# Selection of a gathered tile's experts, moved from the end of the routing into the sweep

## The chip, the cores and the metric

The kernel runs on one core of one Trainium2 chip. The metric is the device time of one execution in microseconds, the median of several runs. TensorE (PE), VectorE (DVE), ScalarE (ACT), GpSimd (POOL) and SyncE (SP) each work through their own instructions in order and wait for one another by semaphores. Weights and tables lie in HBM and come in by DMA, mostly issued on SP's queue; POOL issues the indirect ones.

## The reference, cut to what matters

Two layers, each with four token mixers and then the PEER retrieval, on 256 latent and 256 context tokens of width 1024. PEER is the part that the change touches. Each of 8 heads scores two lists of 128 keys, takes the 16 best of each, forms the 256 sums, takes the 16 best of these and so names 16 of 16384 experts:

```python
def peer(x, wq, keys, u_tab, v_tab):
    t, d = x.shape
    q = (x @ wq).astype(f32).reshape(t, PEER_HEADS, 2, PEER_DK // 2)
    s = jnp.einsum('thpd,hpnd->thpn', q, keys.astype(f32))
    sv, si = lax.top_k(s, PEER_TOPK)
    cand = (sv[:, :, 0, :, None] + sv[:, :, 1, None, :]).reshape(t, PEER_HEADS, PEER_TOPK * PEER_TOPK)
    cidx = (si[:, :, 0, :, None] * PEER_NKEYS + si[:, :, 1, None, :]).reshape(t, PEER_HEADS, PEER_TOPK * PEER_TOPK)
    best, pos = lax.top_k(cand, PEER_TOPK)
    eidx = jnp.take_along_axis(cidx, pos, axis=-1)
    g = jax.nn.softmax(best, axis=-1)
    ...
        act = jax.nn.gelu(jnp.einsum('tkd,td->tk', u_tab[ec].astype(f32), xc.astype(f32)), approximate=False)
        return jnp.einsum('tk,tkd->td', gc * act, v_tab[ec].astype(f32))
```

## The kernel before, in words

Layer 0 has four tiles of 128 tokens. Three of them (384 tokens) go through a dense **sweep** over all 128 blocks of 128 experts: for block j, `u_mm` (L1262) multiplies the tokens with U's block j (24 matmuls, tile names `wh`, `wl`, outputs `po`) and applies Gelu (L1278) into a tile `ga`; `gate` multiplies `ga` by the routing weights G and splits it into `Wh` and `Wl`; `split_v` splits V's block, loaded as `vr`, into `vh` and `vl`; `v_mm` adds the block's 18 products into `mm` and `at` (L1698). Every fp32 operand is a sum of a high part, copied by ACT, and a low part, subtracted by DVE, both in `halves` (L1246); `Wh`, `vh`, `wh` are ACT's, `Wl`, `vl`, `wl` DVE's (L1247, L1248). `wl` and `wh` have 3 buffers each, `vr` has 2, `vh` and `vl` 3, `Wh` and `Wl` 4.

The fourth tile, tile 0, goes through a **gather** (L1311): 128 indirect DMAs from POOL (L1321) fetch one row of U for each of its tokens, by the indices `gix`, into three buffers `grow`, DVE takes the dot product of each row with its token (L1328), and after a Gelu 128 rows of V are gathered and summed (L1330, L1332). The generator `gather` yields after each row. In the sweep, loop j calls it a fixed number of times behind `late`, the DVE split of block j+1's V, so that the rows stand in DVE's queue between the splits.

Ahead of both lies the **routing** (L1599): queries, the lists of the 16 best (`top16`), then per tile `select` and `scatter`. `select(i)` (L1434) yields six times: `lst` (ACT, L1439), the candidates' sums `cand` (DVE, L1442), the best 16 of each head `best` and `pos` (four yields), positions into `ab2`, an Exp on ACT (L1473), then `match` against the numbers `iotar`, twice (L1478 to L1483), and for tile 0 the indices `gix` and weights `gw` (L1493 to L1495). `scatter` makes one-hot operands (`ohA`, `ohB`, `ohC`) and PE builds the weights G block by block (L1560); ACT evacuates them to `gblk` and SP stores them to `gd` (L1564), from where the sweep loads them as `G` (L1664). While the routing runs, U steps of the sweep are worked ahead (`early`, a filler).

Routing of layer 0 ends with the scatter of the last dense tile and, in the kernel before, with tile 0's select:

```python
                fill.add(early(ne))
                if NG:
                    yield from select(0)
```

The tile pool `tk` (L1363) closes with the routing and its memory goes to the sweep's tiles; the pool `sel` stays open in layer 0. What order the instructions take on each engine is decided by a scheduler from the program's order, the buffers and its own estimates; the program's order with `issue_after` is the hand that sets it here. Layer 1 has no gathered tile.

Of the kernel before, what the change touches and what calls it, by code (L numbers as in the profile page):

```python
# [10 lines left out]
F16 = mybir.dt.float16  # L11
# [8 lines left out]
P = 128  # L20
# [253 lines left out]
def body(ctx, tc, I, out, dbg=None):  # L274
# [311 lines left out]
    for l in range(DEPTH):  # L586
# [641 lines left out]
        NG = 0 if last else 1  # L1228
# [66 lines left out]
        def early(upto):  # L1295
            while nu[0] < upto:
                u_next()
                yield
# [58 lines left out]
        gath = gather() if NG else iter(())  # L1357

        g_first = (acc if NG else up.tile([P, NB * 64], F32, name="gfirst"))[:, :NB * 64].rearrange("p (b j t) -> p b j t", j=2, t=32)
        with ExitStack() as tx:  # L1360

            sel = (px if NG else tx).enter_context(tc.tile_pool(name=f"sel{l}", bufs=2))
            tk = tx.enter_context(tc.tile_pool(name=f"tk{l}", bufs=1))  # L1363
# [6 lines left out]
            gparts = gT.bitcast(F16).rearrange("p (t s) -> p t s", s=2)  # L1370
            iota4 = tk.tile([P, P, 4], F16, name="iota4")
            dve.tensor_copy(iota4, iota[:, :, None].to_broadcast([P, P, 4]))
            iotar = tk.tile([P, 16, 8], F16, name="iotar")
            dve.tensor_copy(iotar, iota[:, :16, None].to_broadcast([P, 16, 8]))
            KEYS = tk.tile([P, 1024], F32, name="keys")
            pool.dma_start(KEYS, I['keys'][l])
# [18 lines left out]
            def queries(h, a):  # L1395

                w = un.next('wq')
                ps = mm_tile()
                sl = slice(a - nt, a - nt + 256)
                for k in range(KD):  # L1400
                    o = k * 128
                    mm3(ps[:, :256], (w[0][:, o:o + 128], w[1][:, o:o + 128]), (nh[:, k, sl], nl[:, k, sl]), k == 0, k == KD - 1)
                act.activation(q_of(h, a), ps[:, :256], AF.Copy)
# [169 lines left out]
            def both(a, b, na):  # L1573

                live = True
                for _ in b:
                    for _ in range(na):
                        if live:
                            live = next(a, 0) is None
                    yield  # L1580
                for z, _ in enumerate(a):
                    if z % 3 == 2:
                        yield

            def chain(*gens):
                for g in gens:
                    yield from g

            def queries_of(a):
                for u in range(8):  # L1590
                    queries(u, a)
                    if u % 2:
                        yield
# [5 lines left out]
            def routing():  # L1599


                tiles = (0, 1) if last else (2, 3, 1)
                for u in range(0, 8, 2):
                    queries(u, 256)
                    queries(u + 1, 256)
                    if last and u == 6:
                        fill.add(early(own))
                    yield from lists(tiles[:1 if last else 2], (u, u + 1))
                if last:
                    per_step[0] = 2  # L1610
                    yield from select(0)

                    def rest():
                        yield from lists((1,), range(8))
                        fill.add(early(ne))
                        yield from select(1)
                else:
                    yield from both(queries_of(0), select(2), 1)

                    fill.add(early(own + 2048 // nd))  # L1620
                lo_eng[0] = dve
                for z in range(1, ND):
                    more = lists((tiles[z + 1],), range(8)) if z + 1 < ND else iter(())
                    yield from both(scatter(tiles[z - 1]), rest() if last else chain(select(tiles[z]), more), 3)
                per_step[0] = 1

                v0[:] = [up.tile([P, D], F32, name="grow", bufs=3) for _ in range(3)]
                sp.dma_start(v0[0], I['V'][l, 0])
                end = scatter(tiles[-1], True)
                others = lists((0,), range(8)) if NG else iter(())  # L1630
                for z, _ in enumerate(end):
                    next(others, 0)
                    if z == 8:
                        fill.add(early(ne - 2 if NG else ne))
                    yield
                fill.add(early(ne))
                if NG:
                    yield from select(0)

            for _ in routing():  # L1640
                for _ in range(per_step[0]):
                    fill.step()
            fill.flush()


        with ExitStack() as dx:
# [8 lines left out]
            def load_v(j):  # L1655
                if j < P:
                    vr[j] = dp.tile([P, D], F32, name="vr", bufs=2) if j else v0[0]
                    if j:
                        sp.dma_start(vr[j], I['V'][l, j])
# [73 lines left out]
            for j in range(P):  # L1733
                load_v(j + 2)
                load_g(j + 4)

                while nu[0] < min(P, j + own + (ne - own) * max(0, 64 - j) // 64) and free:
                    u_next()
                gate(j + 1)
                if j == 80:  # L1740
                    assert last or all(z < own for z, _ in gas.values())
                    if last:
                        htok = fin.tile([P, 2, D], F32, name="htok")
                        sp.dma_start(htok, h2.rearrange("q p d -> p q d"))
                    else:
                        sp.dma_start(hT, h2)
                        hT_back.append(j)
                late = split_v(j + 1)
                if j < P - TAIL:
                    for i in range(ND):  # L1750
                        v_mm((j,), i, range(2))
                if last and j >= 40 and j % 4 == 0:
                    next(mrows, 0)
                if last and j == 116:
                    table_for_rstd()
                if last and j == 100:

                    rws = fin.tile([P, 2, D], F32, name="rws")
                    grow = fin.tile([KD, P], F32, name="grow8")
                    ps = mm_tile()  # L1760
                    transpose(ps[:KD, :P], mod[:, 40:48, 1])
                    act.activation(grow, ps[:KD, :P], AF.Copy)
                    grow_d = dr.tile([KD, P], F32, name="grow_d")
                    pool.dma_start(grow_d, grow)
                    for q, x in enumerate((grow_d, I['FG'])):
                        pool.dma_start(rws[:, q], bass.AP(tensor=x.tensor, offset=x.offset, ap=[[0, P], [1, D]]))
                if NG and j < P - 1:

                    with tc.issue_after(late.ins):
                        for _ in range((2 if j > 1 else 0) + (j > 24 and j % 2)):  # L1770
                            if next(gath, 0) is not None:
                                break
                        else:
                            continue
                        for _ in range(2):
                            next(mrows, 0)
# [75 lines left out]
```

## Time and profile before

| | |
|---|---|
| median of 3 runs | 3031.93 us (3028.62 to 3033.39) |
| profiled execution: its time, its span | 3033.08 us, 3031.3 us |
| PE busy | 2933.1 us, 97% |
| DVE busy | 2269.7 us, 75% |
| ACT busy | 1478.8 us, 49% |
| POOL busy | 530.7 us, 18% |
| HBM traffic over the span | 228 GB/s |

Times in the profile are microseconds from the span's start. The scatter of the last tile ends near 836; the sweep's V part of layer 0 begins at 849.59 and goes on to 1815. The profile names an instruction by its line, its engine, its operation and its tiles; what stands in square brackets behind a row is the time that the engine was idle before it, and what ended that.

### The profile page before, as it was taken

How to read it: one execution, taken by the hardware profiler on the slowest of the kernel's cores; microseconds unless marked ns; L12 is line 12 of the kernel's file. 1: busy time of each engine (PE TensorE's matmuls, PEld its weight loads, DVE VectorE, ACT ScalarE, POOL GpSimd, SP SyncE). 2: the span in 40 equal slices, each digit the busy share in tenths (PEclk: the TensorE clock that was granted, in tenths of full speed). 3: DMA queues.
4: the chain of work that ended last, by engine and by line, in shares of the span. 5: the costliest groups of instructions: out<-in, count | busy, mean ns of one | idle time of the engine just before them, and what ended most of it. 6: DMA issues, size and time to landing. Idle time of an engine off the chain costs nothing.

```text
span 3031.3 us, 47486 instructions
## 1 busy us (share of the span) xinstructions
PE 2933.1 (97%) x17500; PEld 2590.3 (85%) x17500; DVE 2269.7 (75%) x4818; ACT 1478.8 (49%) x2603; POOL 530.7 (18%) x394
## 2 busy tenths in 40 slices
PE   8999999998999999999999998999899999999997
PEld 6877777898889999999999986789898988999985
DVE  5765988799878777777787687888699667555545
ACT  5444533559843333333333335465558654555543
POOL 1001100230034444444444102000150000000000
PEclk9999999999999999999999999999999999999999
DMA  7232578556689988988989754367546699766644
GB/s 274 73 104 81 182 232 269 185 189 222 240 297 346 317 314 304 323 321 307 326 305 319 263 187 147 90 194 221 191 147 215 209 305 308 220 209 209 214 141 146
DMA packets 271673, 693.42 MB, mean 229 GB/s; under 512 B 22440, under 2 KB 115120, under 8 KB 270928
## 3 DMA queue, kind: packets, MB, share of 16 engines
q1 hardware_dynamic: 228096, 534.85, 52.9%
q0 software_dynamic: 43344, 155.54, 14.9%
q8 instruction: 137, 2.24, 0.3%
q14 instruction: 96, 0.79, 0.1%
HBM read 630.53 MB, written 59.77 MB: 228 GB/s over the span
## 4 chain that ended last, share of the span: by engine, by line
PE 74%; DVE 13%; DMA 7%; ACT 3%; issue 3%; POOL 0%; SPq 0%; DVEq 0%; ACTq 0%; POOLq 0%
PE mm L1698 12%; PE at L1698 12%; PE po L405 9%; PE po L407 9%; PE po L406 8%; PE mm L405 5%; PE mm L407 5%; PE mm L406 5%; PE at L1560 3%; DMA wraw<-in_W_dram 2%; DMA vr<-in_V_dram 2%; DMA wraw<-in_U_dram 1%; PE at L401 1%; DVE wl L337 1%; DMA grow<-in_UR_dram,gix 1%
## 5 line engine op out<-in xcount | busy, mean ns | idle before, releaser
L405 PE MATMUL po<-nh,wh 128*128 128x384 f32 (+1 forms) x2048 | 637.8, 311 | 4.7 <-ACT wh L1247 2.2
L407 PE MATMUL po<-nh,wl 128*128 128x384 f32 (+1 forms) x2048 | 635.3, 310 | 3.3 <-DVE wl L1248 2.6
L1247 ACT ACTIVATE vh<-vr 128x1024 fp32r<-128x1024 f32 x254 | 269.8, 1062 | 369.2 <-DMA vr<-in_V_dram 339.9
L405 PEld LDWEIGHTS po<-nh,wh 128*128 128x128 f32 x2048 | 390.7, 191 | 14.1 <-ACT wh L1247 2.8
L407 PEld LDWEIGHTS po<-nh,wl 128*128 128x128 f32 x2048 | 390.2, 191 | 5.1 <-DVE wl L1248 3.5
L1248 DVE TENSOR_TENSOR vl<-vr,vh 128x1024 fp32r<-128x1024 f32 x254 | 310.5, 1222 | 110.8 <-ACT vh L1247 110.4
L1247 ACT ACTIVATE wh<-wraw 128x1024 fp32r<-128x1024 f32 x236 | 249.5, 1057 | 287.7 <-PE po L406 251.7
L1248 DVE TENSOR_TENSOR wl<-wraw,wh 128x1024 fp32r<-128x1024 f32 x221 | 269.6, 1222 | 115.0 <-ACT wh L1247 114.9
L405 PE MATMUL mm<-nh,wh 128*128 128x256 f32 (+1 forms) x1056 | 346.6, 330 | 8.0 <-ACT nh L502 3.9
L406 PE MATMUL po<-nl,wh 128*128 128x384 f32 x1024 | 343.7, 336 | 0.0
L407 PE MATMUL mm<-nh,wl 128*128 128x256 f32 (+1 forms) x1056 | 341.7, 325 | 0.8 <-POOL wl L337 0.4
L406 PE MATMUL mm<-nl,wh 128*128 128x256 f32 (+1 forms) x992 | 324.2, 328 | 1.4 <-DVE nl L429 1.2
L336 ACT ACTIVATE wh<-wraw 128x1024 fp32r<-128x1024 f32 x176 | 186.0, 1059 | 276.4 <-PE mm L406 89.8
L406 PE MATMUL po<-nh,wh 128*128 128x256 f32 x1024 | 290.9, 284 | 0.0
L1698 PE MATMUL mm<-vl,Wh 128*128 128x512 f32 x635 | 250.3, 394 | 6.3 <-DVE vl L1248 5.9
L1698 PE MATMUL mm<-vh,Wh 128*128 128x512 f32 x635 | 248.7, 392 | 1.4 <-ACT vh L1247 1.4
L1698 PE MATMUL at<-vh,Wl 128*128 128x512 f32 x635 | 248.5, 391 | 0.0
L1698 PE MATMUL at<-vh,Wh 128*128 128x512 f32 x635 | 248.2, 391 | 0.0
L1698 PE MATMUL mm<-vh,Wl 128*128 128x512 f32 x635 | 247.5, 390 | 0.0
L1698 PE MATMUL at<-vl,Wh 128*128 128x512 f32 x635 | 247.0, 389 | 0.0
L405 PEld LDWEIGHTS mm<-nh,wh 128*128 128x128 f32 x1056 | 203.2, 193 | 34.4 <-issue 5.9
L1332 DVE SCALAR_TENSOR_TENSOR gacc<-grow,gdot,gacc 128x1024 f32<-128x1024 f32 x127 | 162.9, 1283 | 92.5 <-DMA grow<-in_V_dram,gix 91.1
(369 smaller groups left out, 6279.2 us busy)
## 6 DMA issues: line engine op xcount, KB each, us to landing
wraw<-in_U_dram SPq DMA_DIRECT2D x276, 512.0 KB, 4.6
vr<-in_V_dram SPq DMA_DIRECT2D x254, 512.0 KB, 4.6
wraw<-in_W_dram SPq DMA_DIRECT2D x214, 512.0 KB, 3.8
gd<-gblk SPq DMA_DIRECT2D x80, 512.0 KB, 4.3
G<-gd SPq DMA_DIRECT2D x32, 768.0 KB, 7.9
G<-gd SPq DMA_DIRECT2D x32, 512.0 KB, 5.6
grow<-in_W_dram SPq DMA_DIRECT2D x24, 512.0 KB, 4.5
ulo<-wl SPq DMA_DIRECT2D x20, 512.0 KB, 3.6
```

Of the source, the lines that this page charges most:

```text
L336: act.activation(h, r, AF.Copy)
L337: (pool if order[m][1] == 'wq' or order[m][:2] == (1, 'na') and order[m][2] < 2 or order[m][0] == 0 and order[m][1] in ('gate', 'hyn') and ...
L401: pe.transpose(o, i, ident)
L405: pe.matmul(ps, w[0], x[0], start=first, stop=False)
L406: pe.matmul(ps, w[0], x[1], start=False, stop=False)
L407: pe.matmul(ps, w[1], x[0], start=False, stop=last)
L1247: act.activation(h, r, AF.Copy)
L1248: return eng.tensor_tensor(lo, r, h.bitcast(F32), op=ALU.subtract)
L1332: dve.scalar_tensor_tensor(acc, g, dot[:, e:e + 1], acc, op0=ALU.mult, op1=ALU.add)
L1560: pe.matmul(ps4[:, :, z], A[:, :, z], C[:, z, :, h], start=h == 1, stop=h == 0)
L1698: pe.matmul(accs[i][h], w[a][:, i * 128:(i + 1) * 128], v[b][:, h * 512:(h + 1) * 512], start=j == 0 and a + b == 0, stop=j == P - 1 and a ...
```

## The change

It moves tile 0's select out of the routing generator and puts it in front of the gather, as its first steps. The loop of the sweep, which calls the gather twice per block (three times for every other block from 25 on), did so from j = 2; now it does from j = 0, so that select's six yields fall to j = 0 to 2 and the gather begins at j = 3. `iotar`, which select reads, moves from the pool `tk` to `sel`.

```diff
@@ -1370,7 +1370,7 @@
-            iotar = tk.tile([P, 16, 8], F16, name="iotar")
+            iotar = sel.tile([P, 16, 8], F16, name="iotar", bufs=1)
@@ -1634,13 +1634,14 @@
                 fill.add(early(ne))
-                if NG:
-                    yield from select(0)
 
             for _ in routing():
                 for _ in range(per_step[0]):
                     fill.step()
             fill.flush()
+            if NG:
+
+                gath = chain(select(0), gath)
@@ -1767,7 +1768,7 @@
                     with tc.issue_after(late.ins):
-                        for _ in range((2 if j > 1 else 0) + (j > 24 and j % 2)):
+                        for _ in range(2 + (j > 24 and j % 2)):
                             if next(gath, 0) is not None:
```

How this moves instructions is seen at three places (from line 1645 on, lines of the changed kernel are one higher). The first is DVE at the start of the last dense tile's scatter. Before:

```order
L1442 TENSOR_TENSOR cand<-sv 128x8x16
L1383 MAX best<-cand 128x8 x2
L1384 MAX_INDEX pos<-best,cand 128x8
L1385 MATCH_REPLACE rep<-best,cand 128x60
L1384 MAX_INDEX pos<-best,cand 128x8
L1386 MAX best<-rep 128x8
L1383 MAX best<-cand 128x8
L1387 MAX_INDEX pos<-best,rep 128x8
L1384 MAX_INDEX pos<-best,cand 128x8
L1385 MATCH_REPLACE rep<-best,cand 128x60
L1522 TENSOR_TENSOR ohA<-iota_5725,iT 128x1024
L1514 TENSOR_SCALAR gT<-at 128x128
```

Now, at the same place:

```order
L1385 MATCH_REPLACE rep<-sv,mm 128x128
L1386 MAX sv<-rep 128x8
L1387 MAX_INDEX si<-sv,rep 128x8
L1522 TENSOR_TENSOR ohA<-iota_5725,iT 128x1024
L1514 TENSOR_SCALAR gT<-at 128x128
```

The candidates and first best lists of tile 0 no longer stand between tile 0's lists (`sv`, `si`) and the scatter's one-hot operands.

The second place is ACT, where the scatter's last blocks give way to the sweep. Before:

```order
L1562 ACTIVATE gblk<-at 128x128x4 x6
L1439 ACTIVATE lst<-si 128x256
L1562 ACTIVATE gblk<-at 128x128x4 x2
L1256 ACTIVATE wh<-wraw 128x1024
L1566 ACTIVATE gacc<-gblk 128x64
L1278 ACTIVATE hT<-po_9154 128x384
L1247 ACTIVATE wh<-wraw 128x1024 x2
L1473 ACT_TABLE_LOAD
L1473 ACTIVATE best<-best 128x128
L1278 ACT_TABLE_LOAD
L1278 ACTIVATE hT<-po_9196 128x384
L1247 ACTIVATE wh<-wraw 128x1024
```

Now:

```order
L1562 ACTIVATE gblk<-at 128x128x4 x7
L1256 ACTIVATE wh<-wraw 128x1024
L1562 ACTIVATE gblk<-at 128x128x4
L1278 ACTIVATE hT<-po_9135 128x384
L1566 ACTIVATE gacc<-gblk 128x64
L1247 ACTIVATE wh<-wraw 128x1024
L1247 ACTIVATE Wh<-ga 128x384 x2
L1439 ACTIVATE lst<-si 128x256
L1247 ACTIVATE wh<-wraw 128x1024
```

`wh` stands one evacuation earlier, `lst` behind the first two `Wh`, and the Exp with its table loads has left this stretch for one further on.

The third place is DVE's queue from the indices `gix` to the first gathered rows (L1328). Before:

```order
L1493 SCALAR_TENSOR_TENSOR gix<-ij 128x128
L1494 SCALAR_TENSOR_TENSOR gix<-ij 128x128
L1248 TENSOR_TENSOR vl<-vr,vh 128x1024
L1687 TENSOR_TENSOR ga<-ga,G_9298 128x384 x2
L1248 TENSOR_TENSOR wl<-wraw,wh 128x1024
L1248 TENSOR_TENSOR Wl<-ga,Wh 128x384
L1248 TENSOR_TENSOR vl<-vr,vh 128x1024
L1248 TENSOR_TENSOR Wl<-ga,Wh 128x384
L1687 TENSOR_TENSOR ga<-ga,G_9309 128x384
L1248 TENSOR_TENSOR wl<-wraw,wh 128x1024
L1248 TENSOR_TENSOR vl<-vr,vh 128x1024
L1328 SCALAR_TENSOR_TENSOR grow,gdot<-grow,mtok 128x1024 x2
```

Now, from the first gathered rows on (the `vl` ahead of them is V7's, the two in the piece are V8's and V9's, the `wl` is U27's):

```order
L1248 TENSOR_TENSOR vl<-vr,vh 128x1024
L1688 TENSOR_TENSOR ga<-ga,G_9502 128x384
L1248 TENSOR_TENSOR wl<-wraw,wh 128x1024
L1328 SCALAR_TENSOR_TENSOR grow,gdot<-grow,mtok 128x1024 x3
L1248 TENSOR_TENSOR Wl<-ga,Wh 128x384
L1248 TENSOR_TENSOR vl<-vr,vh 128x1024
L1328 SCALAR_TENSOR_TENSOR grow,gdot<-grow,mtok 128x1024
L1688 TENSOR_TENSOR ga<-ga,G_9502 128x384
L1328 SCALAR_TENSOR_TENSOR grow,gdot<-grow,mtok 128x1024
L1248 TENSOR_TENSOR Wl<-ga,Wh 128x384
L1328 SCALAR_TENSOR_TENSOR grow,gdot<-grow,mtok 128x1024
L1248 TENSOR_TENSOR vl<-vr,vh 128x1024
```

The gather's rows start behind V7's split instead of V3's, and they come closer together: behind V9's split two more rows, U27's `wl`, three rows with a gate and a `Wl` between, V10's split, two rows, U28's `wl`, one row and V11's split follow. The order on PE, DVE, ACT and SP away from the end of the routing and the sweep's first dozen blocks, and POOL's altogether, is the same as before.

## Rows read from the trace of the kernel before

**Rows 1.** The page: busy time of each engine, with its share and count.

```profile
PE 2933.1 (97%) x17500; PEld 2590.3 (85%) x17500; DVE 2269.7 (75%) x4818; ACT 1478.8 (49%) x2603; POOL 530.7 (18%) x394
```

**Rows 2.** Windows: span, length, busy PE, PEld, DVE, ACT, POOL; clock, DMA share, GB/s.

```profile
836.00:850.00 14.00, 10.39 (x61) 9.78 (x60) 13.08 (x43) 10.15 (x16) 0.00 (x0) 1.00 0.70 262
850.00:854.00 4.00, 4.00 (x12) 3.11 (x11) 4.00 (x11) 1.85 (x2) 0.00 (x0) 0.57 0.98 310
854.00:870.00 16.00, 16.00 (x77) 13.81 (x77) 8.42 (x12) 7.39 (x10) 10.78 (x3) 1.00 0.98 331
870.00:880.00 10.00, 10.00 (x52) 9.01 (x51) 7.47 (x12) 0.72 (x2) 4.92 (x4) 1.00 0.64 215
...
960.00:1800.00 840.00, 840.00 (x4248) 763.70 (x4247) 644.49 (x816) 299.30 (x410) 306.50 (x228) 1.00 0.87 305
```

**Rows 3.** PE's timeline: start, duration, engine, line, operation, tiles, [idle before, its releaser].

```profile
797.06 1.06 PE L1560 MATMUL at<-ohC,ohA 128*128 128x128 f16 x8 [1.43 <-DVE ohC L1538]
...
838.50 0.44 PE L405 MATMUL po<-nh,wh 128*128 128x384 f32 x1 [1.45 <-ACT wh L1256]
838.78 0.34 PE L406 MATMUL po<-nl,wh 128*128 128x384 f32 x1
838.95 0.34 PE L407 MATMUL po<-nh,wl 128*128 128x384 f32 x1
...
849.59 0.50 PE L1698 MATMUL mm<-grow,Wh 128*128 128x512 f32 x1 [2.15 <-ACT Wh L1247]
...
850.39 0.51 PE L1698 MATMUL at<-grow,Wh 128*128 128x512 f32 x1
...
854.04 0.40 PE L1698 MATMUL mm<-grow,Wh 128*128 128x512 f32 x1
854.27 0.39 PE L1698 MATMUL at<-grow,Wh 128*128 128x512 f32 x1
...
906.60 0.50 PE L1698 MATMUL mm<-vl,Wh 128*128 128x512 f32 x1 [1.43 <-DVE vl L1248]
```

**Rows 4.** DVE's timeline, the selection of tile 0, first step to last.

```profile
790.78 0.27 DVE L1442 TENSOR_TENSOR cand<-sv 128x128 f32<-128x128 f32 x1
...
841.57 0.22 DVE L1456 TENSOR_SCALAR sl<-pos 128x128 uint32<-128x128 uint32 x1
...
847.77 1.22 DVE L1478 TENSOR_TENSOR match<-iotar,ab 128x2048 f16<-128x2048 f16 x1
...
854.11 0.28 DVE L1494 SCALAR_TENSOR_TENSOR gix<-ij 128x128 int32<-128x128 f32 x1
```

**Rows 5.** ACT's timeline, from the scatter's end to the first Wh.

```profile
835.65 0.64 ACT L1439 ACTIVATE lst<-si 128x256 f16<-128x256 uint32 x1
...
837.40 1.05 ACT L1256 ACTIVATE wh<-wraw 128x1024 fp32r<-128x1024 f32 x1
...
849.02 0.94 ACT L1247 ACTIVATE Wh<-ga 128x384 fp32r<-128x384 f32 x2 [1.08 <-DVE match L1478]
```

**Rows 6.** POOL's timeline: the first indirect DMA and one further on.

```profile
854.47 8.86 POOL L1321 DMA_INDIRECT grow<-in_UR_dram,gix  x1 [48.75 <-DVE gix L1494]
...
907.96 1.68 POOL L1321 DMA_INDIRECT grow<-in_UR_dram,gix  x1 [8.54 <-DVE grow L1328]
```

**Rows 7.** DVE's timeline: last split before the gather, rows 1, 4 and 10.

```profile
861.20 1.22 DVE L1248 TENSOR_TENSOR vl<-vr,vh 128x1024 fp32r<-128x1024 f32 x1
...
870.67 1.23 DVE L1328 SCALAR_TENSOR_TENSOR grow<-grow,mtok 128x1024 f32<-128x1024 f32 x1 [8.25 <-DMA grow<-in_UR_dram,gix]
...
877.74 1.22 DVE L1328 SCALAR_TENSOR_TENSOR grow<-grow,mtok 128x1024 f32<-128x1024 f32 x1 [1.71 <-DMA grow<-in_UR_dram,gix]
...
895.77 1.22 DVE L1328 SCALAR_TENSOR_TENSOR grow<-grow,mtok 128x1024 f32<-128x1024 f32 x1
```

**Rows 8.** SP's queue: V's first load (vr1); V's loads from 840 to 900.

```profile
844.71 0.33 SPq L1659 DMA_DIRECT2D vr<-in_V_dram  x1
...
DMA to landing us min/median/max: 3.8/5.9/11.8
```

## The prediction

> **What bounds the kernel now.** I read the page first. TensorE (PE) is busy for 97% of the 3031.3 us span, DVE for 75% and ACT for 49% [rows 1], so work that leaves DVE is worth nothing in itself. A microsecond counts only where PE pauses or runs slowly. Next I read the windows around the end of layer 0's routing and in the sweep behind it. In the long sweep PE is busy for all of 960 to 1800, at full clock, with the DMA engines at 0.87 [rows 2]; what PE loses before that stretch is not made up later, and what it gains is not lost again, unless another wait appears. From 836 to 850 PE was busy for only 10.39 of 14.00 us, and from 850 to 854 the granted clock was 0.57 [rows 2]. That is where the selection of tile 0 runs.
>
> Then I read PE's own timeline for what ended each pause [rows 3]. There are four: 1.43 us before 797.06 (DVE's ohC), 1.45 before 838.50 (ACT's wh), 2.15 before 849.59 (ACT's Wh), 1.43 before 906.60 (DVE's vl). Two rates come from the same group: the U matmuls follow each other 0.17 us apart (838.78, 838.95; I use 0.174, so 24 of them, one U step, take 4.18 us), the V matmuls 0.23 apart (854.04, 854.27; I use 0.232, so 18, one V step, take 4.18). From 850.39 to 854.04 nine intervals took 3.65 us instead of 2.09: the low clock cost 1.56.
>
> **What the change removes.** Each of the first three pauses has the moved selection ahead of it.
> - *797.06.* DVE's first cand additions and best lists of tile 0 stand from 790.78 on [rows 4], ahead of the last scatter's one-hot products; about ten of them at some 0.2 to 0.3 us each, as the 0.27 there, some 2.2 us. In the new order they are gone from there. I take 1.4 of 1.43.
> - *838.50.* ACT copied lst (0.64 at 835.65) and then wh (at 837.40) [rows 5]. In the new order lst is behind wh, and wh stands one block evacuation earlier. The gain lies between lst's 0.64 and the whole 1.45; I take 1.2, since the evacuation counts too.
> - *849.59.* Wh's first split waited 1.08 us for the second match (DVE, 847.77 for 1.22) [rows 4, 5]. Wh reuses the memory of iotar, which match reads; the edit moves iotar to a pool that stays open, so the wait has no ground left. I take all of 2.15.
> - *850 to 854.* The low clock came straight behind the longest of these pauses, and 1.56 with it. The window 836 to 850, which holds the pause of 1.45, has a clock of 1.00 [rows 2]. I take 1.55.
>
> The pause of 1.43 at 906.60 is where V8's low half was late. It doesn't survive as such, because DVE's order there is another; I count its 1.43 as gained and put whatever comes instead into the next part. Sum of the gains: 1.4 + 1.2 + 2.15 + 1.55 + 1.43 = 7.7 us. This is also the cap: nothing else in the stretch has PE waiting.
>
> **What the change adds.** No instruction is added on PE or DVE. The pool of iotar costs nothing by itself, and the two extra calls of the gather loop at j = 0 and 1 are the selection's six steps, so that the gather begins at j = 3 instead of 2; its last row still falls before the sweep's end, where no wait of PE's hangs on it, and I cost that at nothing. ACT's Exp with its table loads now stands between sweep operations, some 3 us on an engine that is busy 10.15 of 14.00 there at the fullest [rows 2]; V5's split is due much later, so nothing waits.
>
> The cost is in DVE's queue at the gather. Before, gix was written at 854.11 [rows 4]. Now it stands behind vl5. The work is timed like this:
> - V0 starts when PE has left the scatter and done 29 U matmuls (5.0 us) instead of 51 and a pause: 840.2, from the same rows with the gains above taken off.
> - vl5 needs V's load chain of two buffers: vr1 issued at 844.71 [rows 8], about 2.4 earlier now since the last scatter ends earlier, then three rounds of load 5.9 [rows 8], ACT's vh 1.05 as wh's [rows 5] and vl 1.22 [rows 7]: 842.3 + 24.5 = 866.8.
> - The index part of the selection, with one wl and two Wl between its steps, took from 841.57 to 854.11 + 0.28, 12.8 us [rows 4]. The new order has a vl there in place of one Wl, 1.22 for some 0.5 (its width is 384 of 1024): 13.4 with the overlap of neighbours. So gix is at 880.2, some 26 us later than before.
> - The first indirect DMA took 8.86 us on POOL [rows 6], and its row was there 16.2 us after its issue, at 870.67 [rows 7]. Taken the same: first row at 880.2 + 0.15 + 16.2 = 896.6. If it lands 5.0 us after the indirect's end and not 7.3, a little quicker than a V load: 894.2.
>
> Before, DVE waited 8.25 us for that first row [rows 7] while PE had cover. Now **eleven gather rows stand between vl7 and vl10**, three in front of vl8, and DVE takes its queue in order. A V split that is ready therefore waits for a gathered row from a table in HBM, over three buffers. Before, six rows came in 18.03 us (877.74 to 895.77 [rows 7]), 3.0 each; as lower bound I take a load of 5.9, as V's, and the 1.22 of use, over three buffers: 2.4. With t the first row's arrival, three rows come close together, and by that pace vl8 is ready at t + 5.4, vl9 at t + 14, vl10 at t + 26 to 28, and wl28, behind thirteen rows, at t + 31 to 35.
>
> PE without any wait would need these at: V8 840.2 + 14 steps of 4.18 = 898.7 (its vl is read by the last 6 of the 18, from 901.5), V10 at 915.5 (vl from 918.3), U28 at 919.6 (its wl 0.35 later, 920.0). wl28 sets the largest delay: it is ready between 894.2 + 31 = 925.2 and 896.6 + 35 = 931.6, so PE loses 5 to 11.6 us there in all (part of it already before V8 and V10). Mid: 8.1. The pause of 2.15 was followed by the low clock, the one of 1.45 was not [rows 2, 3]; the new ones together are longer, so I add one such loss, 1.55 (bounds 0 and 3.1). After vl11, whose row count behind the start is two short of before, the order is as before, and PE has its cover back.
>
> **The sum.** −7.7 + 8.1 + 1.55 = +1.95 on the profiled execution's 3033.08, which lies 1.15 above the median of 3031.93. On the median: 3033.9. From the bounds: −7.7 + 5 + 0 = −2.7 to −7.7 + 11.6 + 3.1 = +7.0.
>
> **A rule against a row.** The first indirect's 8.86 us stands beside 1.68 for one at 907.96 [rows 6], and DVE worked without a pause until vl at 861.20 was done at 862.42 [rows 7], 0.9 before that indirect ended at 863.33. The Trainium skill, "SBUF — State Buffer", section "Who interferes with whom", says: "A DVE instruction with two SBUF inputs contends with a GpSimd instruction that reads SBUF"; by that the indirect, which reads its indices from SBUF, would have waited for DVE, and the sum would be rival 1's. The Trainium skill, "GPSIMD Engine Reference", section "Instruction dispatch", gives about 6 us for the load of a kernel's code at its first call; by that the sum stays as above. The indirect at 907.96 followed DVE's work at once (its idle time ended with DVE's use of a row) and took 1.68, and DVE went on with its splits, so the rows favour a cost that only the first one has; none here shows what that cost is.
>
> **Rivals.**
> 1. *The first indirect was held by DVE.* Now DVE has three wide and two narrow operations left behind gix, 3 × 1.22 + 2 × 0.5 = 4.7 us, and then idles waiting for the row. The indirect would end 0.9 after them, at 885.9 instead of 889.2; t is 3.3 earlier, the wait 4.8, the sum with half a clock loss −7.7 + 4.8 + 0.8 = −2.1: 3029.8. For it: 862.42 against 863.33. Against it: 907.96.
> 2. *Gains without a new wait.* If rows arrive as fast as the queue needs them (the DMA engines stood at 0.64 from 870 to 880 [rows 2]), or V and U run ahead of my count, the wait is 0 to 2.7 and the kernel gains 5 to 7.7: 3024.2 to 3027. For it: my V0 and gix times are sums of several steps. Against it: 3.0 per row with eleven rows is more than three PE steps.
> 3. *Slower: the gather's catching up in DVE's queue.* Place: vl10, wl28 and vl11. If a row takes 3.2 to 3.5 us and the first comes at 896.6 or later, wl28 is ready at 934 to 937, PE loses 14 to 17 us, the clock falls once or twice: +8 to +12, 3040 to 3044. It decides from 13.8 us of lost PE time on, pauses and slow clock together (7.7 plus 0.2% of the time, 6.1, about what a measurement of this kernel can tell from no change). For it: DVE idled 8.25 and 1.71 for rows [rows 7], the first with the DMA engines at 0.98 [rows 2]. Against it: at 3.0 a row wl28 is ready by 931.6.
> 4. *Nothing is taken away.* The pauses at 838.50 and 849.59 stay, because other work of ACT's stands ahead of wh and Wh, and gather and splits collide as little as before: within 2 us, 3032.
>
> **How the numbers follow.** My forecast (−2.7 to +6): 0.45. Rival 1: 0.12. Rival 2: 0.18, of which only the upper half passes 0.2%, so 0.10 for faster with a little from rival 1. Rival 3: 0.17, nearly all past 0.2%, so 0.15 slower. Rival 4: 0.08. Same is the rest, 0.75. The range 3026 to 3041 leaves out the best part of rival 2 and the worse part of rival 3, about 0.1 each.
>
> **What would show it.** Right: in the new profile no PE wait on wh or Wh between 830 and 856 and no slice at 0.57 behind it; V0 near 840; gix near 880 on DVE; the first indirect again some 9 us; DVE idle on grow between 885 and 925, and PE pauses released by DVE's vl or wl between 898 and 932, 5 to 11.6 us in all; from 960 on PE busy throughout, a few us shifted. Wrong: an indirect of 1 to 5 us (rival 1), no PE pause in 898 to 932 (rival 2), pauses over 14 (rival 3), or Wh still late at V0 (rival 4).

## The result, and the profile after

The changed kernel takes 3051.82 us in the median (3042.96 to 3061.56, 8 runs), the kernel before 3028.94 us in the same comparison (3025.73 to 3033.39, 8 runs): a ratio of 1.0075, 95% interval 1.0062 to 1.0087. It is slower by 22.9 us, well beyond the 0.2% that can be told from no change and outside the predicted range. Its runs also lie further apart than those of before here: 18.6 us from lowest to highest, against 7.7. Eight runs say little of that: in later comparisons the kernel before alone spread over 10.3 us in 23 runs and over 14.3 and 14.6 in 30.

The engines do the same work as in [rows 1]; the page of the changed kernel's profile (span 3054.4 us) says:

```profile
PE 2940.2 (96%) x17500; PEld 2594.6 (85%) x17500; DVE 2268.4 (74%) x4818; ACT 1477.1 (48%) x2603; POOL 524.3 (17%) x394
```

The windows that answer to [rows 2], with the columns of those rows, and two further on:

```profile
836.00:850.00 14.00, 14.00 (x93) 13.05 (x92) 5.84 (x9) 8.87 (x16) 0.00 (x0) 1.00 0.71 269
850.00:854.00 4.00, 4.00 (x23) 3.78 (x22) 0.38 (x1) 0.00 (x0) 0.00 (x0) 1.00 1.05 318
900.00:920.00 20.00, 18.64 (x93) 16.34 (x92) 14.51 (x22) 2.91 (x4) 9.73 (x8) 1.00 0.71 241
920.00:940.00 20.00, 16.49 (x78) 14.62 (x77) 14.15 (x22) 4.27 (x6) 8.91 (x8) 0.91 0.88 296
940.00:960.00 20.00, 17.80 (x80) 15.70 (x79) 18.51 (x29) 9.30 (x14) 7.29 (x5) 0.91 0.96 345
960.00:1000.00 40.00, 37.27 (x191) 33.79 (x190) 31.03 (x49) 11.74 (x18) 13.74 (x10) 1.00 0.94 326
1300.00:1360.00 60.00, 53.97 (x261) 48.37 (x260) 41.29 (x47) 20.12 (x29) 23.69 (x18) 0.94 0.91 330
```

From 836 to 854 PE no longer pauses, and the stretch at 0.57 is gone: there the prediction came true. But between 900 and 1000 PE is idle for 9.8 of 100 us, and between 1300 and 1360 for another 6, with a lower clock (0.91, 0.94) in three of the windows. PE's timeline shows what ended these pauses (the rows with a pause alone):

```profile
916.36 0.50 PE L1699 MATMUL mm<-vl,Wh 128*128 128x512 f32 x1 [1.36 <-DVE vl L1248]
928.43 0.80 PE L1699 MATMUL mm<-vl,Wh 128*128 128x512 f32 x1 [3.51 <-DVE vl L1248]
944.28 0.44 PE L405 MATMUL po<-nh,wh 128*128 128x384 f32 x1 [2.20 <-ACT ga L1278]
974.06 0.50 PE L1699 MATMUL mm<-vl,Wh 128*128 128x512 f32 x1 [2.73 <-DVE vl L1248]
1315.36 0.79 PE L1699 MATMUL mm<-vl,Wh 128*128 128x512 f32 x1 [6.03 <-DVE vl L1248]
```

And DVE's timeline shows what the late splits stood behind. The first two lines answer to [rows 4, 7]: the indices are written at 889.62 and the first gathered row is used at 901.05. The next three are V10's split behind a row that DVE waited for. The three from 964.89 on are V15's split, and there DVE waited twice for a load of G and not for a row. The last three are V59's, near 1310:

```profile
889.62 0.28 DVE L1494 SCALAR_TENSOR_TENSOR gix<-ij 128x128 int32<-128x128 f32 x1
...
901.05 1.23 DVE L1328 SCALAR_TENSOR_TENSOR grow<-grow,mtok 128x1024 f32<-128x1024 f32 x1 [6.80 <-DMA grow<-in_UR_dram,gix]
...
924.15 0.55 DVE L1248 TENSOR_TENSOR Wl<-hT,Wh 128x384 fp32r<-128x384 f32 x1
926.00 1.23 DVE L1328 SCALAR_TENSOR_TENSOR grow<-grow,mtok 128x1024 f32<-128x1024 f32 x1 [1.30 <-DMA grow<-in_UR_dram,gix]
...
927.15 1.22 DVE L1248 TENSOR_TENSOR vl<-vr,vh 128x1024 fp32r<-128x1024 f32 x1
...
964.89 1.03 DVE L1688 TENSOR_TENSOR ga<-ga,G 128x384 f32<-128x384 f32 x2 [3.26 <-DMA G<-gd]
...
971.38 0.56 DVE L1688 TENSOR_TENSOR ga<-ga,G 128x384 f32<-128x384 f32 x1 [3.39 <-DMA G<-gd]
...
972.79 1.22 DVE L1248 TENSOR_TENSOR vl<-vr,vh 128x1024 fp32r<-128x1024 f32 x1
...
1304.37 1.22 DVE L1328 SCALAR_TENSOR_TENSOR grow<-grow,mtok 128x1024 f32<-128x1024 f32 x1 [3.31 <-DMA grow<-in_UR_dram,gix]
...
1310.86 1.22 DVE L1328 SCALAR_TENSOR_TENSOR grow<-grow,mtok 128x1024 f32<-128x1024 f32 x1 [5.26 <-DMA grow<-in_UR_dram,gix]
...
1314.09 1.22 DVE L1248 TENSOR_TENSOR vl<-vr,vh 128x1024 fp32r<-128x1024 f32 x1
```

V59's high half had been split by ACT at 1299.87, and its low half came at 1314.09: in between DVE stood in front of two rows that had not landed. The pause at 944.28 came by way of ACT, which also takes its work in order: the Gelu that PE waited for stood behind a `Wh` that waited for DVE's gate (941.80), and the gate stood behind U29's `wl` and the row of 939.51, for which DVE had waited 1.32 us.

```profile
942.38 0.52 ACT L1247 ACTIVATE Wh<-hT 128x384 fp32r<-128x384 f32 x1 [5.43 <-DVE hT L1688]
942.81 1.04 ACT L1247 ACTIVATE wh<-wraw 128x1024 fp32r<-128x1024 f32 x1
943.76 0.47 ACT L1278 ACTIVATE ga<-po 128x384 f32<-128x384 f32 x1
```

**Where the time went.** To compare the profiles I add up, for each stretch, the time from one PE matmul's start to the next, less the median of that time for the same pair of forms (shapes and types of the operands) over all profiles of this study. So pauses and slow clock are both in it, in us of PE time lost. Stretches are marked by the start of a step of V (V3 is V's block 3; "scatter" is the start of the first scatter). The experiments, told below, stand in the same table.

| kernel | scatter to V3 | V3 to V9 | V9 to V16 | V53 to V64 | V64 to V120 |
|---|---|---|---|---|---|
| before | 25.8 | 1.8 | 0.1 | 0.1 | 0.5 |
| changed | 24.5 | 0.2 | 14.1 | 9.9 | 0.5 |
| changed, second profile (e8) | 21.8 | 0.9 | 17.5 | 5.2 | 0.5 |
| e1 iotar's pool alone | 32.8 | 0.0 | 2.4 | 1.8 | 0.5 |
| e2 selection before the sweep | 32.9 | 0.0 | 2.9 | 0.9 | 0.5 |
| e3 late gather | 23.2 | 0.0 | 0.0 | 7.5 | 5.0 |
| e4 fourth buffer | 22.6 | 1.1 | 11.1 | 0.1 | 0.5 |
| e5 second iotar | 19.1 | 0.3 | 19.1 | 0.1 | 0.5 |
| e6 second iotar, spread | 18.6 | 0.0 | 2.7 | 0.1 | 0.5 |
| e7 before, spread | 25.8 | 0.0 | 0.1 | 0.1 | 0.5 |
| e9 changed, spread | 22.8 | 0.0 | 4.9 | 0.1 | 0.5 |
| e10 e6 and a fourth buffer | 18.9 | 0.0 | 0.0 | 0.1 | 0.5 |
| e11 e6 and an early indirect | 18.5 | 0.1 | 2.1 | 0.2 | 4.5 |
| e12 other spread | 18.7 | 0.0 | 0.0 | 0.1 | 10.0 |

Changed less before: −1.3 − 1.6 + 14.0 + 9.8 = 20.9, and the two spans differ by 23.1; the rest of the kernel differs by a few us either way from one profile to the next. The first column comes out without medians, too: from the scatter's first matmul to V3's first, the same 1308 matmuls take 201.99 us before (665.47 to 867.46), 195.36 in e5 and 194.91 in e6. Each row is one execution. The profiles of e1 and e9 are the slowest of their runs (3045.74 and 3036.71 us), that of e11 the fastest (3022.48).

### The profile page after: what moved, and what is told of

It reads as the page before. It is cut to its first block, busy times and chain, and to the rows that moved or that the text cites. A ratio compares the mean times of both kernels' runs of the same rounds, so it can differ in the third digit from the quotient of the medians.

```text
span 3054.4 us, 47468 instructions
## 1 busy us (share of the span) xinstructions
PE 2940.2 (96%) x17500; PEld 2594.6 (85%) x17500; DVE 2268.4 (74%) x4818; ACT 1477.1 (48%) x2603; POOL 524.3 (17%) x394
## 4 chain that ended last, share of the span: by engine, by line
PE 60%; DVE 13%; issue 11%; DMA 7%; POOL 5%; ACT 3%; SPq 0%; POOLq 0%; DVEq 0%; ACTq 0%
PE mm L1699 9%; PE at L1699 9%; PE po L407 7%; PE po L405 7%; PE po L406 7%; POOL grow L1321 5%; PE mm L405 5%; PE mm L406 4%; PE mm L407 4%; PE at L1560 3%; DMA wraw<-in_W_dram 3%; DMA vr<-in_V_dram 2%; DVE wl L337 1%; PE at L401 1%; DMA wraw<-in_U_dram 1%
## 5 line engine op out<-in xcount | busy, mean ns | idle before, releaser
L1328 DVE SCALAR_TENSOR_TENSOR grow<-grow,mtok 128x1024 f32<-128x1024 f32 x128 | 154.5, 1221 | 103.8 <-DMA grow<-in_UR_dram,gix 103.6
```

The lines of the kernel that those rows point to most:

```text
L1328: dve.scalar_tensor_tensor(g, g, 1.0, mtok, op0=ALU.mult, op1=ALU.mult, accum_out=dot[:, e:e + 1])
```

## The experiments

The theories: **Q**, the gathered rows come late and crowded into DVE's queue, and V's splits wait behind them. **R**, the routing's own order is what costs. **S**, it is the selection's DVE work inside the sweep.

**e1, iotar's pool alone** (kernel before, one line changed).

```diff
-            iotar = tk.tile([P, 16, 8], F16, name="iotar")
+            iotar = sel.tile([P, 16, 8], F16, name="iotar", bufs=1)
```

> The kernel before with one edit of the change alone: iotar in the pool that stays open; tile 0's selection stays at the routing's end and the gather begins at j = 2. Theory Q (DVE's queue: in the changed kernel the gathered rows come late and crowded, and V's splits wait behind them): the rows stand as before, so no PE pause on vl beyond the 1.4 us of before; the wait on Wh (2.15 us) and the low clock behind it (1.55) go: 3025 to 3028 where before is 3029. Theory R (the routing's inner order is what costs: list matmuls wait for DVE near 710 and the clock falls there): order of the routing as before, so the same 3025 to 3028. If iotar's place itself is the cost, 3040 or more.

Measured: 3038.16 us against 3031.30 for before, ratio 1.0020 (1.0009 to 1.0031). Theories Q and R had this wrong alike; nearest is the third case, that iotar's place itself costs (3040 or more). The longest waits of PE from 660 to 1000, but for `gblk`, which is told below:

```profile
PE mm L1418 <- DVE rep L1385: 5.5, 3, 2.1
PE mm L1698 <- ACT Wh L1247: 2.4, 1, 2.4
PE at L1560 <- DVE ohC L1538: 2.2, 1, 2.2
PE mm L1698 <- DVE vl L1248: 2.1, 1, 2.1
PE po L405 <- ACT wh L1256: 1.5, 1, 1.5
```

The wait on Wh stays (2.4), so iotar's memory was not its ground: DVE's gate for V0 simply stands behind the selection's steps. New are 5.5 us in which three list matmuls (L1418) wait for DVE. But the scatter's waits for ACT's `gblk` fall at the same time, from 11.4 us in 18 to 6.0 in 9, so PE's idle time grows little: from 660 to 860 it is busy for 183.25 of 200 us before and for 181.84 in e1. Most of the 7.0 us of e1's first column is matmuls at a lower clock: the granted clock is 0.84 from 700 to 720, 0.94 from 720 to 740 and 0.91 from 800 to 820, where it is 1.00 before. The edit of one line shows that iotar's pool is the cause; what it moves first is iotar's copy, which in the pool that stays open comes later. The source line's view, kernel before, changed, and e5 (told below):

```profile
L1374 DVE CAST iotar<-kc x2: 221/221/221, 533.5 to 2188.3; 128x128 f16<-128x128 f32 x2
```

```profile
L1374 DVE CAST iotar<-kc x2: 219/223/227, 599.3 to 2212.9; 128x128 f16<-128x128 f32 x2
```

```profile
L1374 DVE CAST iotar<-kc x2: 218/218/219, 536.5 to 2202.7; 128x128 f16<-128x128 f32 x2
```

The scheduler puts the copy 66 us further on (533.5, now 599.3), and the order of lists, one-hot operands and matmuls in the following scatters comes out differently. PE's timeline of the changed kernel at this place:

```profile
709.78 0.79 PE L1418 MATMUL mm<-keys,hT 64*128 64x128 f32 x2 [1.71 <-DVE rep L1385]
...
718.62 0.93 PE L1418 MATMUL mm<-keys,hT 64*128 64x128 f32 x6 [2.17 <-DVE rep L1385]
```

The granted clock from 700 to 720 was 0.84 there, and 1.00 in the kernel before. Why a later copy gives this order was not followed into the scheduler, and no run separates the copy's time from the rest of the pool's effect.

**e2, selection recorded between routing and sweep** (changed kernel).

```diff
-                gath = chain(select(0), gath)
+                for _ in select(0):
+                    pass
...
-                        for _ in range(2 + (j > 24 and j % 2)):
+                        for _ in range((2 if j > 1 else 0) + (j > 24 and j % 2)):
```

> Selection out of the routing generator, but recorded whole between the routing and the sweep; iotar in the open pool; gather from j = 2 as before. Theory Q: the first rows stand behind V3's and V4's splits, two per split, as before, so PE has no more than about 1.5 us of pauses on vl between 860 and 1000 and none near 1300: 3022 to 3029. Theory R: the routing lacks the selection as in the changed kernel, its lists wait near 710 with the low clock there, so some 4 to 6 us are lost there whatever the gather does: 3030 to 3035.

Measured: 3040.29 us, ratio 1.0034 (1.0020 to 1.0047). That is above both ranges. Loss to V3 as in e1 (32.9), and little behind it (2.9 and 0.9). R's loss is there, larger than R said; Q's is not, since the rows come early again (the first at 877.64, in e1 at 875.49). Moving the code without the gather's start adds nothing clear to what iotar's pool does.

**e3, late gather** (changed kernel).

```diff
-                        for _ in range(2 + (j > 24 and j % 2)):
+                        for _ in range((2 if j < 3 or j > 7 else 0) + (j > 24 and (j % 2 or j % 8 == 0))):
```

> The changed kernel with the gather begun at j = 8 instead of 3, two rows per split as from then on, and a third row also at every eighth block from 32 on to make up for it. Theory Q: no crowd of rows in front of V8 to V11, so PE's pauses between 900 and 1000 fall from 9.8 us to below 3; the rows come later altogether, so the lead of V's splits may still be used up near the 128th row: 3025 to 3042. Theory S (the selection's own DVE work inside the sweep is what delays the splits, rows or not): the pauses stay, 3048 to 3055.

Measured: 3040.32 us, ratio 1.0035 (1.0022 to 1.0047). The loss from V9 to V16 goes from 14.1 to 0.0, with the selection's DVE work where it was: S falls, Q stands for that stretch. But some 12 us (7.5 and 5.0) come back between V53 and V120, where the rows are denser.

**e4, a fourth buffer** (changed kernel; "junk" is unused until the gather is over; `LAG` is 3, so the wait for a row moves one row back, too; the diff in part).

```diff
-            rows = lambda: up.tile([P, D], F32, name="grow", bufs=3)
+            rows = lambda e: more[0].tile([P, D], F32, name="junk", bufs=1) if e % 4 >= 3 else up.tile([P, D], F32, name="grow", bufs=3)
...
-                    if e < 2:
+                    if e < LAG:
```

> The changed kernel with a fourth buffer for the gathered rows (it shares the memory of a tile that is used only after the gather), and the rows' use one further behind their issue. Theory Q with the pace set by three buffers: a row every 2.2 to 2.6 us in place of about 3, DVE's idle time on rows between 890 and 1000 below half of the changed kernel's, PE's pauses there below 4 us, none near 1300: 3024 to 3034. Theories R and S: nothing changes, 3045 to 3055. If HBM or the DMA engines set the pace and not the buffers, no change either.

Measured: 3037.82 us, ratio 1.0020 (1.0008 to 1.0031) where the changed kernel has 1.0075: between the ranges of Q and of R and S. The loss near 1300 is gone and V9 to V12 falls from 11.0 to 3.7, but V12 to V16 rises from 3.1 to 7.4, and there DVE waits for other loads:

```profile
956.97 1.03 DVE L1692 TENSOR_TENSOR ga<-ga,G 128x384 f32<-128x384 f32 x2 [3.22 <-DMA G<-gd]
963.37 0.56 DVE L1692 TENSOR_TENSOR ga<-ga,G 128x384 f32<-128x384 f32 x1 [3.29 <-DMA G<-gd]
```

The fourth buffer takes away waits for rows (20.6 us of DVE's time between 890 and 1000 in the changed kernel, 12.3 here), but not these: the changed kernel waited for the same two loads of G, 3.26 and 3.39 us, and lost 2.73 on V15 behind them. Whether the rows' transfers make G late is not shown; the kernel before waits 6.6 us for G in the same stretch, and there V's splits were far enough ahead that PE did not stop.

**e5, a second iotar** (changed kernel; the routing's stays in its pool).

```diff
-            iotar = sel.tile([P, 16, 8], F16, name="iotar", bufs=1)
+            iotar = tk.tile([P, 16, 8], F16, name="iotar")
...
+                ir = iotar
+                if i < NG:
+                    ir = sel.tile([P, 16, 8], F16, name="iotar0", bufs=1)
+                    dve.tensor_copy(ir, iota[:, :16, None].to_broadcast([P, 16, 8]))
```

> The changed kernel, but iotar stays in the routing's pool for the routing's tiles, and tile 0's selection makes a copy of its own in the open pool. Theory R (iotar's new pool delays its first copy, the scheduler orders the routing anew, and three list matmuls wait there, with the clock low behind): no list matmul waits for rep near 710, 718 and 775, and PE loses 4 to 7 us less before V3; with the crowd of rows unchanged the rest stays: 3043 to 3048 where the changed kernel is at about 3052. If R is false (the routing's loss comes from something else), no difference to the changed kernel: 3050 to 3055.

Measured: 3043.13 us, ratio 1.0054 (1.0037 to 1.0071). No list matmul waits for rep, and PE loses 19.1 to V3 in place of 24.5 or 21.8. Here, too, it is mostly the clock: from 660 to 860 PE is busy for 186.74 us in the changed kernel and 187.27 in e5, but the granted clock of 0.84 and 0.91 from 700 to 740 is 1.00 in e5. R holds beside Q. What is left, 19.1 from V9 to V16, falls where Q has it (V15's 4.6 us again behind two waits for G, 3.07 and 2.91); in this profile nothing is lost near 1300.

**e6, second iotar and spread rows** (e5 with another count of rows per block).

```diff
-                        for _ in range(2 + (j > 24 and j % 2)):
+                        for _ in range((2 if j < 3 or j > 5 else 0) + (j > 12 and (j % 3 == 0 if j < 64 else j % 3 > 0))):
```

> The kernel of the second iotar with the gather begun at j = 6, two rows per block to 12, a third at every third block to 63 and at two of three blocks from 64 on. Theory Q with R: neither the routing's waits nor the crowd in front of V8 to V11; PE loses below 1 us between V3 and V16; with fewer rows in the first half the lead of V's splits lasts past the 128th row: 3020 to 3028 where before is 3031. If late rows alone do the harm (no spreading helps, as their sum in the DMA engines is what counts), losses of 5 or more again between V53 and V100: 3030 to 3038.

Measured: 3025.72 us against 3029.30, ratio 0.9987 (0.9978 to 0.9996): 17 less than e5 by this line, and a little faster than before. The one pause left between V3 and V64 is 2.4 us on vl, in a window (920 to 940) with the DMA engines at 1.02.

**e7, the same spread in the kernel before** (without the pause in the gather's start).

```diff
-                        for _ in range((2 if j > 1 else 0) + (j > 24 and j % 2)):
+                        for _ in range((2 if j > 1 else 0) + (j > 12 and (j % 3 == 0 if j < 64 else j % 3 > 0))):
```

> The kernel before with only the gather's rows spread as in the last kernel (from j = 2, a third row at every third block from 13 to 63 and at two of three blocks from 64 on). Theory Q: the kernel before has no PE loss between V9 and V120 to give back, so nothing changes: 3028 to 3033. If the spread alone were worth something, below 3026; if denser rows behind V64 are harmful, above 3034.

Measured: 3028.16 us, ratio 0.9997 (0.9988 to 1.0007). No difference, as Q has it: the kernel before lost nothing there.

**e8, the changed kernel again** (no edit).

> The changed kernel once more, for a second profile. Theory Q: the pauses on vl between 900 and 1000 come again, 8 to 14 us of PE time with the low clock; the loss near 1300, where the lead is below 1 us, comes in a size that varies, 2 to 12 us. Theory R: the three waits of list matmuls near 710, 718 and 775 come again with the same 1.5 to 2.2 us. If the loss near 1300 was chance, it isn't there.

Measured: 3047.37 us (one run). The pauses between V9 and V16 come again (17.5), the list matmuls wait again (4.2 us in three), but the clock is 1.00 from 700 to 720 this time and 0.91 from 760 to 780. The loss near 1300 comes again, smaller (5.2).

**e9, the changed kernel with the spread of e6** (iotar in the open pool; its edit is e6's, made in the changed kernel).

> The changed kernel with only the spread rows (gather from j = 6, third rows as in the kernel that was faster than before), iotar in the open pool as the change has it. Theories Q and R add: the spread takes away the 14 to 19 us of PE between V9 and V16 but for 3, the routing keeps its three waits of list matmuls: 3029 to 3035, 4 to 9 us above the same kernel with a second iotar (3025.7). If iotar's place is harmless, 3025 to 3027.

Measured: 3029.52 us, ratio 0.9993 (0.9983 to 1.0003), the lower end of what R and Q together gave. Its profile shows the three waits on rep (4.5 us) and a loss of 22.8 to V3, 4.2 more than e6. By the times R's part is not told apart from nothing here: the ratio of e6, 0.9987 (0.9978 to 0.9996), overlaps.

**e10, e6 with the fourth buffer** (e6 with e4's edit).

> The kernel with the second iotar and the spread rows, and a fourth buffer for gathered rows. Theory Q: three buffers are enough once the rows are spread, since no PE pause is left that a row ends but one of about 2.4 us near 930, where the DMA engines are full: 3022 to 3028, the same as without the buffer within 3. If the buffers bound the rows still, 3015 to 3021.

Measured: 3021.51 us against 3031.82, ratio 0.9963 (0.9949 to 0.9978): the fastest kernel of the study, faster than both. No loss between V3 and V64. The expectation that three buffers are enough was wrong, though narrowly: e10 lies 4 us below e6 by the medians, 7 by the ratios to before, whose intervals touch at 0.9978. The table places 2.4 us of that; V24's split is ready 16.3 us ahead of PE here, 7.4 in e6. The windows:

```profile
920.00:940.00 20.00, 20.00 (x100) 17.88 (x99) 18.06 (x30) 6.76 (x9) 5.62 (x4) 1.00 1.03 346
940.00:960.00 20.00, 20.00 (x105) 18.46 (x104) 17.41 (x27) 8.03 (x12) 9.96 (x7) 1.00 0.97 355
960.00:1000.00 40.00, 40.00 (x200) 35.95 (x200) 33.54 (x51) 14.05 (x20) 21.12 (x15) 1.00 1.02 382
```

**e11, an early indirect DMA** (e6 and, before the routing, one more indirect load whose rows are overwritten unread).

```diff
+            warm = up.tile([P, 1], I32, name="warm")
+            dve.memset(warm, 0)
+            pool.indirect_dma_start(out=acc, out_offset=None, in_=I['UR'],
+                                    in_offset=bass.IndirectOffsetOnAxis(ap=warm[:, 0:1], axis=0))
```

> The kernel with the second iotar and the spread rows, and one more indirect DMA of POOL's early in layer 0, before the routing, whose rows are overwritten unread. It adds a transfer of 512 KB where PE has cover. Theory W (a cost of the first call): the first indirect of the gather, 4.5 to 9.8 us so far, takes 1 to 2 us, and the early one takes the long time. Theory D (GpSimd waits until DVE pauses): the gather's first indirect again ends 0.9 us after the end of DVE's unbroken work, 4 us or more. Time: 3021 to 3028 by either.

Measured: 3029.36 us, ratio 0.9994 (0.9983 to 1.0005), above the expected 3021 to 3028 and not told apart from e6 by the intervals. Its profile loses 4.5 us from V64 to V120, where e6, with the same rows per block, loses 0.5. Its point is told in the last section.

**e12, another spread** (e6 with one row per block to 11, three of four from 64 on).

```diff
-                        for _ in range((2 if j < 3 or j > 5 else 0) + (j > 12 and (j % 3 == 0 if j < 64 else j % 3 > 0))):
+                        for _ in range(2 if j < 3 else 0 if j < 6 else 1 if j < 12 else 2 + (j > 12 and (j % 3 == 0 if j < 64 else j % 4 > 0))):
```

> The kernel with the second iotar and another spread: from j = 6 one row per block to 11, two from 12, a third at every third block to 63 and at three of four blocks from 64 on. Theory Q: the pause of 2.4 us near 930 goes (fewer rows beside V's and U's loads), at the price of denser rows behind V64, where the lead was 5 us or more: 3021 to 3027. If the denser rows empty the lead, losses of 3 or more between V64 and V110: 3028 to 3034.

Measured: 3036.27 us, ratio 1.0011 (1.0000 to 1.0021), above both ranges. The pause near 930 goes (0.0 from V9 to V16), but behind V80 wl and vl come late (10.0 us from V64 to V120): what is not gathered early must be gathered late, and there is a densest pace for that, too. How much of the 10 us is the spread's is open, since e11, with e6's rows, lost 4.5 there.

## Why the prediction was wrong

The sum had gains of 7.7, a wait of 8.1 with 1.55 of slow clock behind it, and nothing after V11. The profiles show gains of 2.9 (1.3 to V3, 1.6 to V9), a loss of 14.0 from V9 to V16 and one of 9.8 near 1300. Three steps failed: that iotar's pool costs nothing, that the wait and its slow clock come to 9.65 us, and that PE has its cover back after V11.

- **The gains** were read rightly, but the changed kernel does not keep them. The four losses ahead of V3 were put at 1.4 + 1.2 + 2.15 + 1.55 = 6.3 us. With the routing's iotar in its old pool (e5, e6) that stretch loses 19.1 and 18.6 instead of 25.8: 6.7 and 7.2. The fifth, 1.43 at V8, came too (V3 to V9: 1.8, now 0.2). One ground was wrong: Wh did not wait for iotar's memory (e1), it stood behind the selection.
- **"The pool of iotar costs nothing by itself"** failed. It cost 7.0 us to V3 in e1 and 2.7 to 5.4 in the changed kernel (21.8 and 24.5 against 19.1). The section on the change also said that the order away from the routing's end was the same as before; it had changed from iotar's copy on, through all of layer 0's scatters.
- **gix** was put at 880.2 and came at 889.6 (885.5 in e8); V5's split, ahead of it, was put at 866.8 and ended at 876.5. Of these 9.4 us 2.2 lie ahead of the routing's scatter (its first matmul at 667.69, before at 665.47), and 7.2 go with iotar's pool: counted from that matmul gix was put at 214.7 us and came at 221.9, but at 215.7 in e5 and 215.0 in e6, so V's loads and splits had been reckoned rightly. The first row was put at 896.6 and came at 901.05; the first indirect, 5.19 us and not 8.86, gave back 3.7.
- **The wait behind the rows**: the mechanism was right, the term 8.1 + 1.55 was too small. PE lost 14.1, 17.5 and 19.1 in the three profiles with the crowd and three buffers. The pace of the rows was forecast rightly: with the first row at t, V8's, V10's and U28's splits were put at t + 5.4, t + 26 to 28 and t + 31 to 35, and ended at t + 5.4, t + 27.3 and t + 31.2. Three other things were not. First, the low half of V is read from the third of its step's 18 matmuls on, not by the last 6 (V10 begins at 924.30 and stands at its third, 928.43); V9 and V10 paused, and when PE came to U28, its low half was ready. Second, behind V11 two pauses were not in the sum, 2.20 by way of ACT's Gelu and 2.73 at V15, behind late loads of G. Third, the clock fell to 0.91 from 920 to 960: of the 14.1 us 9.8 are pauses and 4.3 slower matmuls, where I had 1.55 and at most 3.1.
- **"PE has its cover back" after V11** failed, and this is also the 9.9 us near 1300. The lead of V's splits (first use of vl on PE less the end of its split) was worn down in both kernels over V31 to V59, as each block adds two or three rows:

| | V31 | V45 | V53 | V59 |
|---|---|---|---|---|
| before | 15.9 | 9.4 | 7.0 | 3.6 |
| changed | 11.2 | 0.8 | 0.1 | 0.1 |

The kernel before came to the 128th row with 3.6 us in hand; the changed one had spent them, and two late rows (3.31 and 5.26 us of DVE's time) stopped PE for 6.03. How much that costs differs from one execution to the next (9.9 and 5.2 in the two profiles; 0.1 in e5, whose lead at V59 was 1.8). That the smaller lead at V31 is the whole cause is not shown: e1 and e2 had 16.7 and 17.1 there, more than before, and stood at 0.1 at V59 all the same, with losses of 1.8 and 0.9. What the runs do show is that the loss near 1300 goes away with a fourth buffer (e4) or with the rows spread (e6, e9), which kept 8.6 us or more in hand at V59.

Rival 3 was the nearest: its place, DVE's queue at V10 and on, and its sign were right, and its decisive 13.8 us of lost PE time were passed (14.1 from V9 to V16 alone). Its ground was not met: it wanted a row every 3.2 to 3.5 us, and the first thirteen followed each other 2.4 us apart (901.05 to 929.86). I gave it 0.17 because I took the pace of rows before as the measure and did not look at what the lead is used for later.

## What to carry to other kernels

A generator that is moved moves everything behind it: look where the work that now starts later has to catch up, and whether an engine that takes its queue in order has other things behind it there. Where a margin is built up early and spent late, read it along the whole stage, not only at the change; here nothing was left of it at V59, and PE lost 5 to 10 us some 400 us behind the change. And moving one small tile to another pool moved its first write by 66 us and the order of a whole stage with it: compare the order of the instructions from that write on, not only at the place that was meant.

## What the runs showed that I had not expected

The first indirect DMA took 8.86 us before [rows 6], and I favoured a cost of the first call. In the changed kernel POOL's and DVE's rows were

```profile
889.97 5.19 POOL L1321 DMA_INDIRECT grow<-in_UR_dram,gix  x1 [78.78 <-DVE gix L1494]
```

```profile
893.03 1.22 DVE L1248 TENSOR_TENSOR wl<-wraw,wh 128x1024 fp32r<-128x1024 f32 x1
```

It ended at 895.16, 0.91 after DVE's unbroken work (894.25). Before, it was 0.91, too (863.33, 862.42). In all thirteen profiles without another indirect ahead of it the difference is the same 0.91, with durations from 4.51 to 9.80 us. In e11 an earlier indirect had already run, and took 1.06 us:

```profile
532.82 1.06 POOL L1359 DMA_INDIRECT gacc<-in_UR_dram,warm  x1 [8.60 <-DVE warm L1358]
...
880.09 4.49 POOL L1321 DMA_INDIRECT grow<-in_UR_dram,gix  x1 [76.99 <-DVE gix L1502]
```

```profile
532.77 0.22 DVE L1378 CAST iotar<-kc 128x128 f16<-128x128 f32 x1
...
883.15 0.55 DVE L1696 TENSOR_TENSOR ga<-ga,G 128x384 f32<-128x384 f32 x1
```

The gather's first still ended (884.58) 0.9 after the end of DVE's last operation before its pause (883.70). The early one, too, ended (533.88) 0.89 after DVE fell idle (532.99), and that was 0.2 us after its start. So it was rival 1's mechanism, GpSimd held until DVE pauses, and not a first call. In e3 a pause of 0.62 us was enough: DVE stopped at 893.04, the indirect ended at 893.95. The Trainium skill, "SBUF — State Buffer", section "Who interferes with whom", has it that a DVE instruction with two SBUF inputs contends with a GpSimd instruction that reads SBUF; the 0.91 of the first indirect agrees with that. The load of code at a first call, which the Trainium skill's "GPSIMD Engine Reference" gives as about 6 us in its section "Instruction dispatch", does not show here: 1.06 us. Later indirects are not held in this way, though they read the same indices: one of the changed kernel at 917.72 took 1.68 us while DVE worked without a pause until 919.74, and none of the later ones took over 2 us in any profile. Why the first alone is held stays open.
